# SBUF laid out anew: weight parts and moving operands at fixed places modulo 256 bytes

## The chip, the core and the metric

The kernel runs on one core of a Trainium2 chip. The metric is the device time of one execution in microseconds (us). Within the core, PE (TensorE) multiplies matrices, PEld is its weight-load side, DVE (VectorE) and ACT (ScalarE) do elementwise work, POOL (GpSimd) does a few fills, and SP (SyncE) issues the DMAs. SBUF is the on-chip memory; a place in it is given here as a byte address within each of its 128 partitions, mostly modulo 256.

## What is computed

A two-layer transformer block is followed by a second block with a convolution, a gated delta rule and one more feed-forward part, on 256 tokens of width 1024, in float32. Only the large matrix products matter here; in the reference they are plain `@`:

```python
def first_block(x, ...):
    for layer in range(DEPTH):                       # 2 layers
        xn = rms_norm(h, norm_mix_g[layer])
        mix = even_mixer(...) if layer % 2 == 0 else odd_mixer(...)   # attention, xn @ w_in, y @ w_out
        h = h + mix
        h = h + conv_gated_ffn(rms_norm(h, norm_ffn_g[layer]), ...)   # x @ w_up, conv, silu(g) * u, @ w_down
    return rms_norm(h, norm_out_g)

def second_block(x, p, ...):
    proj = h @ w_in                                  # conv branch, q, k, v, z, gates
    ...                                              # depthwise conv, gated delta rule, two output gates
    x = x + y @ w_o[i]
    x = x + (jax.nn.silu(gt) * up) @ w_down[i]       # second feed-forward part
    pl = rms_norm_2(p[i] @ w_pl_proj[i], ...)
    x = x + jax.nn.sigmoid(rms_norm_2(x, ...) @ w_pl_gate[i]) * pl
    return rms_norm_2(x, g_final)
```

## The kernel before

**Weights.** All large weights come from one flat array, piece by piece (mostly 1 MB: 8 blocks of 128 rows by 256 columns). `Weights.raw` issues the DMA into a buffer `raw`. `Weights.new` then makes two parts of it: `hi` is the piece rounded to float32r by ACT (L208), `lo` is the rest, raw minus hi, by DVE (L209). Each kind has two buffers in a pool of its own (`raw`, `hi`, `lo`); in most stages `W.more` adds a third `hi` and `lo` from the stage's pool.

**Products.** Activations are split in the same way by `split_into`; a tile such as `xs0` has for each of its blocks 256 columns of hi and 256 columns of lo. `mmA` makes three matmuls of 256 columns for each block: x-hi with weight-hi, x-lo with weight-hi, x-hi with weight-lo. There the weight part is the stationary operand (128x128, loaded by PEld before each matmul) and the activation is the moving one (256 columns). `mmB`, used by `nat`, by the last gate (`mmF`) and by `pl_proj` (`mmP`), has it the other way round: the activation stands and the weight part moves. A few pieces (`NATIVE`) are multiplied unsplit, `hg` moving against `raw`. All go through `mm`, so the profile has them on L265.

**Tiles that move in `mmA`.** `xs1` (the normalised input of the feed-forward parts and of the in-projection of the second block; the attention output in `out_proj`, there called `mmO`), `xs0` (the input of the mixers, and the unnormalised input of the first two column pairs of a feed-forward part with convolution), `hid` (the hidden layer, moving in the down product, `mmD`), `yd0`, `yd1` and `yos` (outputs of the delta rule and of the gates). `mmU` is the up product.

**Stages.** In the trace they run one after another: even mixer (1 to 148.5 us), up and down product of layer 0 (148.5 to 274.8 to 339.2), odd mixer (to 449.9), up and down of layer 1 (to 577.3 to 641.7), the second block's mixer (to 1031.8), its up and down product (to 1162.6 to 1227.1) and the last gate (to the end). The order of instructions is that of the code; it has no scheduler.

**Places.** A pool takes SBUF in the order in which pools are opened, and a tile lies behind the tile that was first asked for before it in its pool. Nothing pads them, so a tile's place modulo 256 is what the tiles before it add up to.

Of the kernel before, what the change touches and what calls it, by code (L numbers as in the profile page):

```python
# [10 lines left out]
F32 = mybir.dt.float32  # L11
FR = mybir.dt.float32r
# [39 lines left out]
def weight_spec():  # L52

    w8 = lambda n, cols: [(n, 0, 8, c, 256) for c in cols]
    halves = lambda n, k0: [(n, k0, 4, 0, 512), (n, k0, 4, 512, 512)]
    s = [("even_in", 0, 8, 1792, 68)] + w8("even_in", (1536, 1860, 2116, 2372, 2628, 2884, 3140))
    s += w8("even_in", (0, 256, 512, 768, 1024, 1280))
    s += halves("even_out", 4) + halves("even_out", 0)
    s += up_down("up0", "down0")
    s += w8("odd_in", (1544,)) + [("odd_in", 0, 8, 1536, 8)] + w8("odd_in", (1800, 2056)) + w8("odd_in", range(0, 1536, 256))  # L60
    s += halves("odd_out", 4) + halves("odd_out", 0)
    s += up_down("up1", "down1")
    first = {"g": "ba", "k": "k", "p": "qv", "z": "z", "x": "x", "y": "y"}
    col = {"a": 0, "b": 1024, "q": 2048, "k": 3072, "v": 4096, "z": 5120, "x": 6176, "y": 7200}
    piece = lambda key: w8("in2", [col[key[0]] + 256 * int(key[1])])
    for q in SEQ:
        if q[0] == "r":
            s += piece(q[1:])
        for c in first.get(q[0], ""):
            if "r" + c + q[1] not in SEQ:  # L70
                s += piece(c + q[1])
        if q == "e":
            s += [("in2", 0, 8, 6144, 32)]
        if q == "o":
            s += w8("delta_out", range(0, 1024, 256))
    s += w8("conv_out", range(0, 1024, 256))
    s += w8("o", range(0, 1024, 256))
    u = up_down("up2", "down2")
    s += u[:2] + [("pl_proj", 0, 2, 0, 1024)] + u[2:]
    s += w8("pl_gate", range(0, 1024, 256))  # L80
    return s
# [132 lines left out]
def emit(ctx, tc, A):  # L214
    nc = tc.nc
    V, S, PE = nc.vector, nc.scalar, nc.tensor
    pool = lambda name, bufs, **k: ctx.enter_context(tc.tile_pool(name=name, bufs=bufs, **k))
    cp, sp = pool("cp", 1), pool("sp", 1)
    W = Weights(nc, A["wts"], weight_spec(), pool("raw", 2), pool("hi", 2), pool("lo", 2))
    banks = {}  # L220

    def phase(stack, name, tags):
# [18 lines left out]
    h = cp.tile([128, 8, T], F32, name="h")  # L241
    for k in range(0, 8, 2):
        nc.sync.dma_start(h[:, k:k + 2], A["xT"][:, k:k + 2])
    hgp = pool("hgp", 1)
    hg = hgp.tile([128, 8, T], F32, tag="hg", name="hg")
    xp = pool("xp", 1)
    new_xs = lambda: xp.tile([128, 8, 512], FR, tag="xs0", name="xs0")
    xs1 = cp.tile([128, 8, 512], FR, name="xs1")
    acc = cp.tile([128, T], F32, name="acc")
    ones = cp.tile([128, 128], F32, name="ones")  # L250
    V.memset(ones, 1.0)
# [7 lines left out]
    C = {n: cst[:, o:o + w] for n, (o, w) in coff.items()}  # L259
    Pm = {n: gain[:, o:o + w] if o < NGAIN else par[:, o - NGAIN:o - NGAIN + w] for n, (o, w) in poff.items()}  # L260
    ident = C["ident"]


    def mm(out, lhsT, rhs, start=True, stop=True):
# [53 lines left out]
    def small(n, name, bufs=2):  # L318
        return sp.tile([128, n], F32, tag=name, name=name, bufs=bufs)
# [46 lines left out]
    def rstd_cols(*parts, eps=EPS):  # L366
        m, r = small(2, "rm"), small(2, "rs", 3)
        V.tensor_scalar(m, mean_cols(*parts), eps, None, OP.add)
        rsqrt(r, m, 2)
        return r  # L370

    def rstd_row(r):
        t = sp.tile([128, T], F32, tag="rsb", name="rsb", bufs=2)
        S.copy(t, row_bcast(r, "rb"))
        return t
# [17 lines left out]
    def pieces_A(name, xs, n, use, parts=None):  # L393

        for i in range(n):
            w = W.split(name, parts or P_ODD)
            ps = bank("mm", "mmA")
# [11 lines left out]
    def ffn(up, dn, g, conv, beside=None):  # L409
        with ExitStack() as st:  # L410
            fp = st.enter_context(tc.tile_pool(name=up, bufs=1))
            if XF:
                W.more(fp, XF, XR if conv is not None else 0)
                st.callback(lambda: setattr(W, "extra", None))
            phase(st, up + "p", {"mm": 6, "t": 2})
            def scale(dst, ps):

                V.tensor_tensor(dst.rearrange("p (m t) -> p m t", m=2), ps.rearrange("p (m t) -> p m t", m=2),
                                rb[:, None, :].to_broadcast([128, 2, T]), OP.mult)


            xu = xs1 if conv is None else new_xs()
            for k in range(8):
                split_into(xu[:, k], h[:, k], g[:, k:k + 1])
            rb = rstd_row(rstd_cols(acc))
            hid = fp.tile([128, 22, 512], FR, tag="hid", name="hid")
            for i in range(11):
                src = []
                first = i < NU and conv is not None
                for q in range(2):  # L430
                    ps = bank("mm", "mmU")
                    w = W.split(up, P_UP)
                    for m in range(2):
                        mmA(ps[:, T * m:T * m + T], w, xu if first else xs1, m)
                    src.append(ps)
                if i == 0 and beside is not None:
                    beside()
                if first and i == 0:
                    for k in range(8):
                        t = sp.tile([128, T], F32, tag="xh", name="xh", bufs=2)  # L440
                        V.scalar_tensor_tensor(t, h[:, k], g[:, k:k + 1], rb, OP.mult, OP.mult)
                        split_into(xs1[:, k], t)
                if first or conv is None:
                    for q in range(2):
                        t = fp.tile([128, 512], F32, tag=f"cv{q}" if conv is None else "sil", name="uns", bufs=2)
                        scale(t, src[q])
                        src[q] = t
                if conv is not None:
                    cw, cb = conv
                    for q in range(2):  # L450
                        a = fp.tile([128, 512], F32, tag=f"cv{q}", name="cv", bufs=2)
                        for m in range(2):
                            ch = 22 * q + 2 * i + m
                            x, y = src[q][:, T * m:T * m + T], a[:, T * m:T * m + T]
                            S.activation(y, x, AF.Identity, bias=cb[:, ch:ch + 1], scale=cw[:, 3 * ch + 2:3 * ch + 3])  # L455
                            for d in (1, 2):
                                V.scalar_tensor_tensor(y[:, d:], x[:, :T - d], cw[:, 3 * ch + 2 - d:3 * ch + 3 - d],  # L457
                                                       y[:, d:], OP.mult, OP.add)
                        src[q] = a
                s = fp.tile([128, 512], F32, tag="sil", name="sil", bufs=2)  # L460
                S.activation(s, src[0], AF.Silu)
                V.tensor_tensor(s, s, src[1], OP.mult)
                s3 = s.rearrange("p (m t) -> p m t", m=2)
                hh = hid[:, 2 * i:2 * i + 2]
                S.copy(hh[:, :, :T], s3)
                V.tensor_tensor(hh[:, :, T:], s3, hh[:, :, :T].bitcast(F32), OP.subtract)
            for i in range(4):
                ps = bank("mm", "mmD")
                k0 = 0
                for a in range(3):  # L470
                    w = W.split(dn, P_DN)

                    for m in range(2):
                        mmA(ps[:, T * m:T * m + T], w, hid, m, k0, a == 0 and m == 0, a == 2)
                    k0 += w[0].shape[1]
                residual(i, halves(ps))


    def few_columns(name, n, xs, raw, w, t, use):


        raw = W.raw(name, raw[:, :8 * n])
        w = w[:, :16 * n].rearrange("p (k n) -> p k n", k=8)
# [177 lines left out]

    with ExitStack() as st:
        ap = st.enter_context(tc.tile_pool(name="ev", bufs=1))
        if XE:
            W.more(ap, XE)
            st.callback(lambda: setattr(W, "extra", None))
# [135 lines left out]

    with ExitStack() as st:
        ap = st.enter_context(tc.tile_pool(name="od", bufs=1))
        if XO:
            W.more(ap, XO)
            st.callback(lambda: setattr(W, "extra", None))
# [90 lines left out]
    with ExitStack() as st:  # L898
# [442 lines left out]
        yds = {}  # L1341

        def yd(hd):
            if not yds:
                dls.close()
                yds["p"] = st.enter_context(tc.tile_pool(name="dq", bufs=1))
                yds[0] = hgp.tile([128, 4, 512], FR, tag="hg", name="yd0")
                yds[1] = yds["p"].tile([128, 4, 512], FR, name="yd1")
            return yds[hd // 4][:, hd % 4]
# [225 lines left out]
```

## Time and profile before

| | us |
|---|---|
| median of 3 timed runs | 1268.67 |
| all three | 1268.9, 1263.83, 1268.67 |
| the profiled execution, as timed | 1263.23 |
| its span from first to last instruction | 1261.4 |

| engine | busy us | share of span | instructions |
|---|---|---|---|
| PE | 1229.7 | 97% | 10452 |
| PEld | 1179.9 | 94% | 10452 |
| DVE | 974.5 | 77% | 1920 |
| ACT | 712.3 | 56% | 1178 |

How to read it: matmuls are pipelined, so the length that the profile gives for one (some 280 ns) is not what it costs. In a dense row of matmuls the cost of one is the distance from its start to the next start, which is read from the starts in the timeline, or from a stretch of the chain of waits divided by its count. The mean granted clock of TensorE is 0.991 of full speed; in the stages of the feed-forward parts it is 1.00 throughout.

### The profile page before, as it was taken

What the parts mean: (1) busy time and instruction counts of PE and PEld (TensorE: products, weight loads), DVE (VectorE), ACT (ScalarE), POOL (GpSimd) and SP (SyncE); (2) the same over time, 40 slices, a digit from 0 to 9 for tenths busy, and PEclk for the clock granted to TensorE, in tenths of its full rate; (3) what the DMA queues carried; (4) which work ended last, traced back from release to release, by engine and by line L of the source; (5) the groups of instructions that cost most, each with busy time, mean ns of one, the idle gap of its engine ahead of it and who ended that gap; (6) DMA issues with size and microseconds to landing.
All of it is one profiled execution on the core that took longest, in us unless ns stands there. A gap on an engine that the chain in (4) does not pass through costs nothing.

```text
span 1261.4 us, 25071 instructions
## 1 busy us (share of the span) xinstructions
PE 1229.7 (97%) x10452; PEld 1179.9 (94%) x10452; DVE 974.5 (77%) x1920; ACT 712.3 (56%) x1178; POOL 11.6 (1%) x21
## 2 busy tenths in 40 slices
PE   8999999999999999999999999999999999999997
PEld 8988999999989889999989998989999999999997
DVE  6977699885586689887559898899997778666546
ACT  4566566564365566565425488889544555444433
POOL 0000000000000000000010000000000000000000
PEclk8999999999999999999999999999999999999998
DMA  6543355555343254545425233112143555545542
GB/s 244 198 148 148 132 203 181 190 181 184 127 149 134 101 201 167 201 167 193 151 97 179 104 127 135 68 39 98 68 168 134 183 212 199 199 174 188 184 165 78
DMA packets 29345, 195.43 MB, mean 155 GB/s; under 512 B 3504, under 2 KB 4016, under 8 KB 9136
## 3 DMA queue, kind: packets, MB, share of 16 engines
q1 hardware_dynamic: 29232, 193.83, 43.2%
q8 instruction: 82, 1.34, 0.4%
q14 instruction: 31, 0.25, 0.1%
HBM read 192.77 MB, written 1.05 MB: 154 GB/s over the span
## 4 chain that ended last, share of the span: by engine, by line
PE 74%; issue 11%; DVE 4%; ACT 3%; POOL 1%; POOLq 0%; ACTq 0%; DVEq 0%
PE mmU L265 29%; PE mmD L265 15%; PE mmA L265 12%; PE mmB L265 3%; PE mmO L265 3%; PE mmF L265 2%; DVE lo L209 1%; PE sr L265 1%; ACT hi L208 1%; PE do L265 1%; PE at_y L265 1%; PE at_t L268 1%; PE at_s L265 1%; PE mc L265 0%; PE mmP L265 0%
## 5 line engine op out<-in xcount | busy, mean ns | idle before, releaser
L208 ACT CAST hi<-raw 128x1024 fp32r<-128x1024 f32 (+2 forms) x273 | 336.4, 1252 | 296.9 <-PE mmU L265 114.1
L209 DVE TENSOR_TENSOR lo<-raw,hi 128x1024 fp32r<-128x1024 f32 (+2 forms) x273 | 399.9, 1476 | 110.7 <-ACT hi L208 109.4
L265 PE MATMUL mmU<-xs,hi 128*128 128x256 f32 x2112 | 374.2, 280 | 4.4 <-DVE h L390 4.4
L265 PEld LDWEIGHTS mmU<-xs,hi 128*128 128x128 f32 x2112 | 323.8, 188 | 5.2 <-issue 3.1
L265 PE MATMUL mmU<-xs,lo 128*128 128x256 f32 x1056 | 296.5, 281 | 1.9 <-DVE lo L209 1.9
L265 PE MATMUL mmA<-xs,hi 128*128 128x256 f32 x1152 | 223.2, 290 | 0.2 <-ACT hi L208 0.2
L265 PEld LDWEIGHTS mmU<-xs,lo 128*128 128x128 f32 x1056 | 198.7, 188 | 2.4 <-DVE lo L209 2.3
L265 PE MATMUL mmD<-hid,hi 128*128 128x256 f32 x1056 | 190.2, 283 | 0.0
L265 PEld LDWEIGHTS mmA<-xs,hi 128*128 128x128 f32 x1152 | 181.3, 191 | 1.8 <-issue 0.5
L265 PE MATMUL mmA<-xs,lo 128*128 128x256 f32 x576 | 165.8, 288 | 1.2 <-DVE lo L209 1.2
L265 PEld LDWEIGHTS mmD<-hid,hi 128*128 128x128 f32 x1056 | 164.7, 192 | 0.0
L265 PE MATMUL mmD<-hid,lo 128*128 128x256 f32 x528 | 149.4, 283 | 0.0
L265 PEld LDWEIGHTS mmA<-xs,lo 128*128 128x128 f32 x576 | 109.8, 191 | 2.9 <-DVE lo L209 1.4
L1302 DVE SCALAR_TENSOR_TENSOR cv<-cpad,par,cv 128x256 f32<-128x256 f32 x240 | 107.9, 480 | 0.5
L265 PEld LDWEIGHTS mmD<-hid,lo 128*128 128x128 f32 x528 | 101.4, 192 | 0.0
L265 PE MATMUL mmB<-hi,xs 128*128 128x256 f32 x416 | 77.5, 284 | 0.9 <-DVE h L390 0.9
L457 DVE SCALAR_TENSOR_TENSOR cv<-mmU,par,cv 128x255 f32<-128x255 f32 (+1 forms) x144 | 65.1, 478 | 11.4 <-ACT cv L455 10.3
L265 PEld LDWEIGHTS mmB<-hi,xs 128*128 128x128 f32 x416 | 64.8, 190 | 1.9 <-issue 1.5
L265 PE MATMUL mmA<-hg,raw 128*128 128x256 f32 x256 | 64.5, 388 | 0.9 <-PE mmD L265 0.9
L265 PE MATMUL mmB<-lo,xs 128*128 128x256 f32 x208 | 59.1, 284 | 0.0
L265 PEld LDWEIGHTS mmA<-hg,raw 128*128 128x128 f32 x256 | 46.0, 191 | 6.1 <-PE mmD L265 1.1
L455 ACT ACTIVATE cv<-mmU,par 128x256 f32<-128x256 f32 x72 | 38.6, 558 | 20.0 <-DVE cv L457 20.0
(449 smaller groups left out, 1725.3 us busy)
## 6 DMA issues: line engine op xcount, KB each, us to landing
raw<-in_wts_dram SPq DMA_DIRECT2D x157, 1024.0 KB, 4.8
raw<-in_wts_dram SPq DMA_DIRECT2D x24, 896.0 KB, 4.5
at_l<-in_relb_dram SPq DMA_DIRECT2D x4, 384.0 KB, 9.1
h<-in_xT_dram SPq DMA_DIRECT2D x4, 256.0 KB, 3.9
out_dram<-xg SPq DMA_DIRECT2D x2, 512.0 KB, 2.6
cst<-in_cst_dram SPq DMA_DIRECT2D x1, 640.0 KB, 8.8
buf<-in_g_plp_dram SPq DMA_DIRECT2D x1, 512.0 KB, 5.0
gfin<-in_g_fin_dram SPq DMA_DIRECT2D x1, 512.0 KB, 5.2
```

The lines of the kernel that those rows point to most:

```text
L208: self.nc.scalar.copy(hi[:, a:b], r[:, a:b])
L209: self.nc.vector.tensor_tensor(lo[:, a:b], r[:, a:b], hi[:, a:b].bitcast(F32), OP.subtract)
L265: PE.matmul(out, lhsT=lhsT, rhs=rhs, start=start, stop=stop, skip_group_check=True)
L268: PE.transpose(out, in_, ident)
L455: S.activation(y, x, AF.Identity, bias=cb[:, ch:ch + 1], scale=cw[:, 3 * ch + 2:3 * ch + 3])
L457: V.scalar_tensor_tensor(y[:, d:], x[:, :T - d], cw[:, 3 * ch + 2 - d:3 * ch + 3 - d], y[:, d:], OP.mult, OP.add)
L1302: V.scalar_tensor_tensor(cv[:, k], cpad[:, k, t:t + T], cw[:, t:t + 1], cv[:, k], OP.mult, OP.add)
```

## The change

It adds `gap`, which asks a pool for a tile that nobody uses, and opens the pools in another order: the weight pools `raw`, `hi`, `lo` first, then `xp` and `hgp`, then `cp` and `sp`. `xs1` moves from `cp` to `xp`. Gaps stand before `hid`, before the first tile of the stage pools `ev`, `od` and `dq`, and elsewhere. No computation is added, removed or altered. In the built program each engine has the same instructions in the same order, with the same semaphores and the same values waited for; what differs is the addresses.

```diff
@@ emit
-    cp, sp = pool("cp", 1), pool("sp", 1)
+
+    def gap(p, n, name):
+
+        if n:
+            p.tile([128, n // 4], F32, tag=name, name=name)
+
+
     W = Weights(nc, A["wts"], weight_spec(), pool("raw", 2), pool("hi", 2), pool("lo", 2))
+    xp, hgp, cp, sp = pool("xp", 1), pool("hgp", 1), pool("cp", 1), pool("sp", 1)
+    gap(xp, 192, "xs_gap")
...
-    hgp = pool("hgp", 1)
     hg = hgp.tile([128, 8, T], F32, tag="hg", name="hg")
-    xp = pool("xp", 1)
     new_xs = lambda: xp.tile([128, 8, 512], FR, tag="xs0", name="xs0")
-    xs1 = cp.tile([128, 8, 512], FR, name="xs1")
+    xs1 = xp.tile([128, 8, 512], FR, name="xs1")
...
+    gap(sp, 96, "sp_gap")
@@ ffn
             rb = rstd_row(rstd_cols(acc))
+            gap(fp, 192, "hid_gap")
             hid = fp.tile([128, 22, 512], FR, tag="hid", name="hid")
+            gap(fp, 64, "hid_gap2")
@@ even mixer
         ap = st.enter_context(tc.tile_pool(name="ev", bufs=1))
+        gap(ap, 224, "ev_gap")
@@ odd mixer
         ap = st.enter_context(tc.tile_pool(name="od", bufs=1))
+        gap(ap, 192, "od_gap")
@@ second block, yd
                 yds["p"] = st.enter_context(tc.tile_pool(name="dq", bufs=1))
+                gap(yds["p"], 224, "dq_gap")
```

The places modulo 256 that the two built programs have:

| tile | before | after |
|---|---|---|
| `raw`, `hi`, `lo` of the pools | 96 | 128 |
| third `hi`, `lo` in the feed-forward parts | 96 | 128 |
| third `hi`, `lo` in the even, odd mixer | 128, 160 | 128, 128 |
| `xs0`, `hg`, `yd0` | 96 | 64 |
| `xs1` | 128 | 64 |
| `hid` | 96 | 64 |
| `yd1`, `yos` | 64 | 64 |

All steps inside these tiles are multiples of 256 bytes, so the distance between a moving and a stationary operand is the same, modulo 256, for all matmuls of a tile pair. Counted over the 8064 float32r matmuls of 256 columns in pieces (moving place minus stationary place):

| distance before | distance after | matmuls |
|---|---|---|
| +32 | -64 | 4224 (2784 `mmU`, 1152 `mmA`, 288 `mmO`) |
| 0 | -64 | 2592 (1584 `mmD`, 384 `mmU`, 576 `mmA`, 48 `mmO`) |
| -32 | -64 | 384 (288 `mmA` on `yd1` and `yos`, 48 `mmA`, 48 `mmO`) |
| -64 | -64 | 48 (`mmA`, one piece of the odd mixer) |
| 0 | +64 | 576 (384 `mmB`, 192 `mmF`) |
| +32 | +64 | 144 (`mmB`) |
| +64 | +64 | 96 (`mmB`) |

## Rows read from the trace of the kernel before

**Rows 1.** The page's busy times: engine, us (share of span) xinstructions.

```profile
PE 1229.7 (97%) x10452; PEld 1179.9 (94%) x10452; DVE 974.5 (77%) x1920; ACT 712.3 (56%) x1178; POOL 11.6 (1%) x21
```

**Rows 2.** The page's chain that ended last, by engine and by line.

```profile
PE 74%; issue 11%; DVE 4%; ACT 3%; POOL 1%; POOLq 0%; ACTq 0%; DVEq 0%
PE mmU L265 29%; PE mmD L265 15%; PE mmA L265 12%; PE mmB L265 3%; PE mmO L265 3%; PE mmF L265 2%; DVE lo L209 1%; PE sr L265 1%; ACT hi L208 1%; PE do L265 1%; PE at_y L265 1%; PE at_t L268 1%; PE at_s L265 1%; PE mc L265 0%; PE mmP L265 0%
```

**Rows 3.** Chain in six dense stretches: start us, us, what xcount.

```profile
279.95 20.16 PE mmD L265 x168
...
394.94 5.40 PE mmA L265 x45
400.33 5.28 PE mmB L265 x44
...
179.99 90.10 PE mmU L265 x765
...
1059.99 90.07 PE mmU L265 x772
...
1011.97 16.09 PE mmA L265 x136
```

**Rows 4.** Groups kept apart by shape: names, shapes xcount | busy us, mean ns | idle.

```profile
L265 PE MATMUL mmU<-xs,hi 128*128 128x256 f32 x2112 | 374.2, 280 | 4.4 <-DVE h L390 4.4
L265 PE MATMUL mmD<-hid,hi 128*128 128x256 f32 x1056 | 190.2, 283 | 0.0
L265 PE MATMUL mmA<-hg,raw 128*128 128x256 f32 x256 | 64.5, 388 | 0.9 <-PE mmD L265 0.9
```

**Rows 5.** PE timeline, odd mixer, distance -64: start us, us, line, names, xcount.

```profile
387.09 0.39 PE L265 MATMUL mmA<-xs,hi 128*128 128x256 f32 x2
387.32 0.28 PE L265 MATMUL mmA<-xs,lo 128*128 128x256 f32 x1
387.43 0.39 PE L265 MATMUL mmA<-xs,hi 128*128 128x256 f32 x2
...
388.11 0.39 PE L265 MATMUL mmA<-xs,hi 128*128 128x256 f32 x2
...
390.10 0.28 PE L265 MATMUL mmA<-xs,lo 128*128 128x256 f32 x1
390.21 0.40 PE L265 MATMUL mmA<-xs,hi 128*128 128x256 f32 x2
390.45 0.28 PE L265 MATMUL mmA<-xs,lo 128*128 128x256 f32 x1
...
391.61 0.28 PE L265 MATMUL mmA<-xs,lo 128*128 128x256 f32 x1
391.72 0.39 PE L265 MATMUL mmA<-xs,hi 128*128 128x256 f32 x2
391.95 0.28 PE L265 MATMUL mmA<-xs,lo 128*128 128x256 f32 x1
...
392.65 0.40 PE L265 MATMUL mmA<-xs,hi 128*128 128x256 f32 x2
...
394.06 0.40 PE L265 MATMUL mmA<-xs,hi 128*128 128x256 f32 x2
```

**Rows 6.** PE timeline, odd mixer, weight part moving at distance +64.

```profile
356.65 0.40 PE L265 MATMUL mmB<-hi,xs 128*128 128x256 f32 x2
...
357.71 0.40 PE L265 MATMUL mmB<-hi,xs 128*128 128x256 f32 x2
```

**Rows 7.** Busy by stage: from:to, us, PE PEld DVE ACT POOL (x), clock, DMA, GB/s.

```profile
148.50:274.80 126.30, 126.28 (x1063) 125.93 (x1064) 111.49 (x173) 79.59 (x101) 0.00 (x0) 1.00 0.52 185
...
641.70:1031.80 390.10, 384.18 (x3512) 359.06 (x3512) 338.88 (x779) 251.15 (x450) 10.31 (x16) 0.99 0.35 123
```

**Rows 8.** PE's waits: who for whom, us in total, times, longest us.

```profile
PE mmU L265 <- DVE lo L209: 1.9, 2, 1.3
PE mmA L265 <- DVE lo L209: 1.2, 1, 1.2
```

## The prediction

> **What bounds the kernel now.** I read the busy times first: PE has work for 97% of the span and its weight loads for 94%, DVE for 77% [rows 1]. The chain that ended last says the same by cause: 74% of it is PE, and six groups of large products alone (mmU, mmD, mmA, mmB, mmO, mmF) make 64% [rows 2]. PE hardly waits for the weight parts; the two largest such waits are 1.9 and 1.2 us in all [rows 8]. So the kernel's time is, for the most part, a number of matmuls times the distance between their starts.
>
> That distance is the thing to look at. All of these matmuls have one form (128x128 weights, 256 columns), yet their distance differs by place. In the down product 168 take 20.16 us, 120.0 ns each. In the odd mixer mmA and mmB, in pieces at distance 0 as well, take 5.40/45 and 5.28/44, again 120.0. In the up product of layer 0, at +32, it is 90.10/765 = 117.8; in the up product of the second block, at +32 too, 90.07/772 = 116.7; on `yos`, at -32, 16.09/136 = 118.3 [rows 3]. The profile's own lengths follow (280 ns for mmU, 283 for mmD), though they are no cost [rows 4]. The distance 0 is the dearest, in two stages and with either operand as the weight. I take it that the two operand streams of PE hinder each other depending on their places modulo 256. The trace does not show the mechanism, only that the cost goes with the place.
>
> One piece of the odd mixer happens to have the new distance, -64. There, in the stretch from 387.09 to 388.11, 9 matmuls take 1.02 us, 113.3 ns each. After an interruption the same piece takes 0.35 us for three (390.10 to 390.45), 117; after another 0.34 for three (391.61 to 391.95), 113; after a third 1.41 us for twelve (392.65 to 394.06), 117.5 [rows 5]. So -64 has two rates: a fast one that no other distance holds for long, and a slow one near what +32 has now. Within a dense stretch neither changed into the other; an interruption changed it. The long stretches behave likewise: mmU at +32 holds 117.8 over 765 matmuls in one stage and 116.7 over 772 in another [rows 3].
>
> **The change part by part.** No instruction, order or wait changes, and the built program has the gaps where they were meant, so there is nothing to add or remove but nanoseconds per matmul. I cost each group at both rates of -64, the slow one taken as 117.8 (it lies between 117 and 118, and the +32 row of 117.8 has far more matmuls), the fast one as 113.3. Gains in us, slow and fast:
>
> mmD, 1584 from 120.0: 2.2 ns or 6.7 ns each, 3.5 or 10.6. The 384 mmU on `xs0` and 624 mmA and mmO at distance 0: 0.8 or 2.6, and 1.4 or 4.2. mmU on `xs1` in layers 0 and 1, 1728 from 117.8: 0 or 7.8. mmU in the second block, 1056 from 116.7: a loss of 1.2, or 3.6. The 1440 mmA and mmO at +32, which sit between 116.7 and 117.8 and for which I take 117.2: a loss of 0.9, or 5.6. The 384 from -32 and 118.3: 0.2 or 1.9. mmB and mmF swap their roles, so they go to +64, not -64: one row shows it, 1.06 us for nine, 117.8 [rows 6], so 576 from 120.0 gain 1.3 either way, and 144 from +32 nothing. The unsplit products (256 halves on `hg` and `raw`, [rows 4]) stand at 0 and go to -64; their half-rate stream has no second distance in this trace, so I bound them by 256 times the 6.7 ns between 120.0 and 113.3, 1.7 us either way, and take nothing.
>
> The feed-forward parts thus give 3.5 + 0.8 + 0 - 1.2 = 3.1 us if all are slow and 10.6 + 2.6 + 7.8 + 3.6 = 24.6 if all are fast. The mixers and the last gate give 1.4 - 0.9 + 0.2 + 1.3 = 2.0 or 4.2 + 5.6 + 1.9 + 1.3 = 13.0. The first sum lies on the path whole: mmU and mmD are 44% of the chain, 555 us [rows 2], and their 4752 matmuls take 3168 times 117.6 and 1584 times 120.0, 563 us. What hides the preparation is slack on DVE: in the up product of layer 0 it is busy 111.5 of 126.3 us [rows 7]. If PE finishes that stage in 121.5 us, at the fast rate, DVE still has 10 us to spare; were that cover gone, the gain there would stop at those 111.5. In the mixers DVE is busy 338.9 of 390.1 us in the longest one [rows 7], and softmax, the delta rule and convolution stand in the same chains, so I pass on 0.7 of the second sum: 1.4 or 9.1.
>
> A rule speaks against all this. PE's two streams give 120.0 and 113.3 ns for the same tiles at different places [rows 3, 5], which looks like one disturbing the other. The Trainium skill, page "TensorE: Matmul & The Clock Gate", section "Step-by-step: what each phase is for", says that TensorE has two independent read ports into SBUF and that "Loading the next tile's weights doesn't steal SBUF read bandwidth from the running matmul." By that rule the sum of this change would be 0; this trace does not agree with it, since the distance of starts follows the places.
>
> Half of the possible: the four dense stretches at -64 were two fast and two slow. That makes (3.1 + 24.6)/2 + (1.4 + 9.1)/2 = 13.9 + 5.3 = 19.2 us. Against the profiled execution, 1263.2 us as timed (1.8 of it outside the span), that is 1244. The median of the runs is 5.4 higher, 1268.7, and gives 1249.5; of the three timed runs and the profiled one, two lie at each end. I take the middle, 1247.
>
> **The rivals.** *Nearly all fast*, 24.6 + 9.1 to 13.0 = 34 to 38 us, 1226 to 1235, middle 1231. For it: the fast rate appears at once after an interruption, and a stretch without stalls, such as 800 matmuls of an up product and the down product behind it, may keep it to its end. Against it: half of what is seen is slow.
>
> *Nearly all slow*, 3.1 + 1.4 = 4.5 us, 1259 to 1264, middle 1261. For it: +64 and +32 show 117.8 in many stretches, so that rate seems to be one that any distance but 0 can hold. Then only the removal of distance 0 pays.
>
> *Places decide nothing*, 1263 to 1269. For it: each distance goes with certain tiles and stages, so something else of them might set the rate, such as what the other engines do there. The sentence quoted above from the Trainium skill, page "TensorE: Matmul & The Clock Gate", would have it so. Against it: at distance 0 two stages and both roles show the same 120.0 [rows 3].
>
> *Slower: -64 sinks to a third, worse rate.* The longest dense stretch at -64 in the rows is twelve matmuls [rows 5]. Should it, held longer, fall to the 120.0 that distance 0 holds for 168 and more, then 1728 lose 2.2 ns, 1056 lose 3.3, 1440 lose 2.8 and 384 lose 1.7: 3.8 + 3.5 + 4.0 + 0.7 = 12.0, less the 1.3 of mmB and mmF, 10.7 us. That is 1274 to 1279. It decides where a stretch lasts much longer than that, that is in all feed-forward parts. Against it: neither rate drifts within the stretches seen.
>
> **How the numbers follow.** Chances: a mixture as forecast, 0.52; nearly all fast 0.18; nearly all slow 0.14; places decide nothing 0.06; slower 0.10. About 0.5%, 6 us, is what a measurement of this kernel can tell from no change. The mixture is faster by more than that in nearly all its spread: with one, two or three of the three feed-forward parts fast it gives about 16, 23 or 30 us, with none 8. Nearly all slow, at 4.5 us, falls on the line, so I give a third of it to faster. Faster 0.52 + 0.18 + 0.05 = 0.75, the same 0.09 + 0.06 = 0.15, slower 0.10. The range reaches from the middle of nearly all fast, 1231, to the upper end of nearly all slow, 1264; it leaves out half of 0.18 below and the slower case and part of "nothing" above. The mixture alone spans 1235 to 1260.
>
> **What the changed profile would show.** The same instruction counts on every engine and the same waits. In the down products, starts 113.3 or 117.8 ns apart, each kept over hundreds of matmuls, where 120.0 stands now. In the up products, long stretches at 113.3 in at least one of the three. mmB and mmF at 117.8. The profile's length of an mmD matmul falls below 283 ns [rows 4]. I am wrong if mmD still shows 120, if stretches at -64 drift, or if the starts come closer while PE begins to wait for `lo` from DVE, over the 3 us of now [rows 8].

## The result, and the profile after

The changed kernel takes 1254.03 us in the median of three executions (1247.33 to 1255.93), beside 1268.30 us for the kernel before in the same series; the ratio is 0.9883, 95% interval 0.9855 to 0.9912. A fourth execution of that series took 3035.48 us at full granted clock and is left out; no run shows why. A second series gave 1251.87 (nine executions, 1249.54 to 1260.39) beside 1265.27, ratio 0.9920 [0.9894, 0.9945]. So it is about 1% faster, 14.3 and 13.4 us by medians, where 19.2 had been forecast against the profiled execution. The first profiled execution, 1255.93 us with a span of 1254.1, is 7.3 us below the one of before.

The page's busy times, as in [rows 1]:

```profile
PE 1221.4 (97%) x10452; PEld 1170.0 (93%) x10452; DVE 974.2 (78%) x1920; ACT 713.6 (57%) x1178; POOL 11.6 (1%) x21
```

The counts are those of before; PE is 8.3 us less busy, its weight-load side 9.9, and the other engines differ by at most 1.3. An mmD matmul is 279 ns long by the profile, 283 before [rows 4], and PE's waits for `lo` are 1.8 us, 3.1 before [rows 8]; names as there:

```profile
L274 PE MATMUL mmD<-hid,hi 128*128 128x256 f32 x1056 | 184.4, 279 | 0.0
...
PE mmA L274 <- DVE lo L209: 1.1, 1, 1.1
...
PE mmU L274 <- DVE lo L209: 0.7, 1, 0.7
```

Where the starts lie is read from the chain that ended last, in its dense stretches, as in [rows 3] (start us, us, what, xcount):

```profile
179.94 92.93 PE mmU L274 x820
272.88 59.85 PE mmD L274 x528
...
457.91 113.18 PE mmU L274 x961
571.09 62.20 PE mmD L274 x528
...
1045.92 110.95 PE mmU L274 x942
1156.86 62.20 PE mmD L274 x528
```

All six stretches now stand at distance -64. In layer 0 it is 92.93/820 = 113.3 ns and 59.85/528 = 113.4, in layer 1 and in the second block 117.8 in each. The 120.0 of the down product has gone from all three layers. One of three feed-forward parts is at the fast pace, two at the slow one, each from the last interruption in its up product (177.8, 455.0 and 1043.6 us) to its end. The first pieces, before that, stand at either pace. The unsplit products, for which nothing was taken, stand at 216 ns before and after.

The stages of the feed-forward parts and of the second block's mixer, as in [rows 7] (from:to, us, busy PE PEld DVE ACT POOL, granted clock, DMA share, GB/s), first profile of after:

```profile
148.80:272.70 123.90, 123.47 (x1062) 123.00 (x1063) 110.91 (x172) 79.24 (x101) 0.00 (x0) 0.99 0.53 188
272.70:333.70 61.00, 60.06 (x531) 59.90 (x529) 35.12 (x48) 28.02 (x38) 0.31 (x1) 1.00 0.51 177
...
443.70:570.90 127.20, 127.13 (x1062) 126.80 (x1063) 112.28 (x175) 79.29 (x103) 0.00 (x0) 0.99 0.53 189
570.90:634.20 63.30, 62.41 (x531) 62.23 (x529) 33.32 (x50) 25.43 (x37) 0.81 (x1) 1.00 0.43 153
634.20:1025.00 390.80, 384.35 (x3513) 358.59 (x3513) 338.90 (x779) 251.81 (x450) 10.29 (x16) 0.99 0.35 123
1025.00:1156.70 131.70, 130.96 (x1086) 129.56 (x1087) 92.73 (x116) 60.08 (x60) 0.00 (x0) 1.00 0.55 190
```

Up and down product of layer 0 give 2.4 and 3.4 us, those of the other two 0.2, 1.1, -0.9 and 1.2: 7.4. The mixers and the gate give nothing in this execution (-0.1). One reason is the clock. Windows of the same view, in this profile:

```profile
150.20:153.60 3.40, 3.40 (x19) 3.40 (x18) 3.32 (x6) 3.40 (x2) 0.00 (x0) 0.52 0.03 7
443.80:447.20 3.40, 3.40 (x16) 3.29 (x17) 3.40 (x6) 3.40 (x7) 0.00 (x0) 0.51 0.62 260
706.60:713.40 6.80, 6.80 (x31) 6.53 (x31) 4.60 (x15) 2.59 (x5) 0.00 (x0) 0.51 0.00 0
```

There the granted clock was at the lower of its two levels (1.2 GHz), and matmuls started 213 ns apart. A further window of 3.4 us stands at 952.5. In the profile of before the lower level stands, in these stages, at 715.8 and at 958.1, 3.4 us each, and not at the start of the up products. The first window followed a wait of PE for `h` from DVE of 1.93 us; the second profile below has that same wait and no fall. And the first kernel under Experiments, whose up products stand where they stood before, has a window at the start of layer 1's (448.1 us). So I put it down to the execution, not to the change.

### The profile page after: what moved, and what is told of

Its sections match the earlier page's. It is cut to its first block, busy times and chain, and to the rows that moved or that the text cites. A ratio compares the mean times of both kernels' runs of the same rounds, so it can differ in the third digit from the quotient of the medians.

```text
span 1254.1 us, 25071 instructions
## 1 busy us (share of the span) xinstructions
PE 1221.4 (97%) x10452; PEld 1170.0 (93%) x10452; DVE 974.2 (78%) x1920; ACT 713.6 (57%) x1178; POOL 11.6 (1%) x21
## 4 chain that ended last, share of the span: by engine, by line
PE 72%; issue 12%; DVE 5%; ACT 3%; POOL 1%; POOLq 0%; ACTq 0%; DVEq 0%
PE mmU L274 28%; PE mmD L274 15%; PE mmA L274 12%; PE mmO L274 3%; PE mmB L274 3%; DVE lo L209 2%; PE mmF L274 2%; PE sr L274 1%; ACT hi L208 1%; PE do L274 1%; PE at_y L274 1%; PE at_t L277 1%; PE at_s L274 1%; PE mc L274 1%; ACT xbd L1191 0%
## 5 line engine op out<-in xcount | busy, mean ns | idle before, releaser
L274 PEld LDWEIGHTS mmU<-xs,lo 128*128 128x128 f32 x1056 | 202.2, 192 | 1.4 <-DVE lo L209 1.2
L274 PE MATMUL mmD<-hid,hi 128*128 128x256 f32 x1056 | 184.4, 279 | 0.0
L274 PEld LDWEIGHTS mmD<-hid,hi 128*128 128x128 f32 x1056 | 160.4, 188 | 0.0
```

The lines of the kernel that those rows point to most:

```text
L274: PE.matmul(out, lhsT=lhsT, rhs=rhs, start=start, stop=stop, skip_group_check=True)
```

## Experiments

In all of them the pace is the distance between the starts of 256-column float32r matmuls. "Fast" is 113.3 ns, "slow" 117.8. Where no spread and no interval stands beside a time, the kernel was executed once.

**One part of the change alone.** The kernel before, with gaps round `hid` only; all else as before, so the up products stay at distance 0 and +32.

```diff
+            fp.tile([128, 48], F32, tag="hid_gap", name="hid_gap")
             hid = fp.tile([128, 22, 512], FR, tag="hid", name="hid")
+            fp.tile([128, 16], F32, tag="hid_gap2", name="hid_gap2")
```

> The kernel before with one part of the change: hid alone moves, from 0 to -64 against the weights; xs1, xs0 and all else stay. If the distance sets the rate: mmD leaves 120.0 ns between starts and shows 113.3 or 117.8 in each of the three down products; mmU on xs1 stays at 117.8 or 116.7, mmA at distance 0 at 120.0; the time falls by 3.5 us (all slow) to 10.6 us (all fast). If something else of the new layout sets it (the absolute places of weights, the order of the pools): mmD stays at 120.0 and the time within 0.5%.

1255.88 us beside 1265.71. The chain, down products of layer 0, layer 1 and the second block (the middle one from 577.94 on):

```profile
276.24 59.87 PE mmD L265 x528
...
577.94 54.17 PE mmD L265 x478
...
1156.64 62.20 PE mmD L265 x528
```

113.4, 113.3 and 117.8, where before they stand at 120.0 ([rows 3] for layer 0; the stages of the other two are as long). The long stretches of the up products stay at 117.8, 118.0 and 116.7. Moving one tile, with the same instructions around it, moved the pace of its matmuls and of no other: this shows that the place decides.

**Distance or place.** After, with every tile 128 bytes higher, so the weight parts at 0 and the moving operands at 192.

```diff
+    gap(W.rawp, 64, "shift")
     xp, hgp, cp, sp = pool("xp", 1), pool("hgp", 1), pool("cp", 1), pool("sp", 1)
```

> The changed kernel with every tile 128 bytes higher: weights at 0 modulo 256, moving operands at 192, the distance still -64. If only the distance counts: the same two rates, 113.3 and 117.8 ns, in the same kinds of stretches, none at 120.0 or 116.7; which stretch gets which may differ; time 1240 to 1260 us. If the absolute place counts: other rates, or 120.0 again.

1246.51 us. The same two paces and no other: layers 0 and 1 fast, the second block slow (62.08 us for 527). The distance counts; the places themselves, shifted together, bring no new pace. One shift was tried; with the two kernels above, -64 has now shown the same two paces at three pairs of places (`hid` against weight parts: 32 and 96, 64 and 128, 192 and 0).

**Other distances, with a break ahead of each piece.** A 1-column float32 matmul, called a kick here (its result is not used), ahead of each of the 102 feed-forward weight pieces, to enter each piece anew. `hid` at -48, -80 and -64 in the three parts, `xs0` and `xs1` at -64.

```diff
+            def kick():
+                mm(bank("t", "kick")[:, 0:1], ones, ones[:, 0:1])
...
                     w = W.split(up, P_UP)
+                    kick()
```

> The changed kernel with one extra matmul of a single column ahead of each weight piece of the feed-forward parts (102 in all, some 0.2 us each with its refill, 15 to 25 us more), so that each piece of 48, 42 or 96 matmuls starts anew. hid stands at -48, -80 and -64 in the three parts. If the phase at the start of a stretch picks between two rates that then hold: the pieces of an up product, all alike in places, are a mixture of 113.3 and 117.8, each piece at one rate, where the changed kernel had some 1400 matmuls at one rate. If the rate belongs to the stage (its other engines, its buffers): all pieces of one stage keep that stage's rate. -48 and -80 show whether steps of 16 bytes matter: the same pair of rates if not.

1277.63 us. The chain of the second block's down product, at -64 (a float32 kick shows as x2; pieces have 42 or 48 matmuls):

```profile
1187.93 4.89 PE mmD L274 x42
1192.82 0.12 PE kick L274 x2
1192.94 5.76 PE mmD L274 x48
1198.70 0.12 PE kick L274 x2
1198.82 4.89 PE mmD L274 x42
1203.71 0.12 PE kick L274 x2
1203.82 5.06 PE mmD L274 x42
1208.88 0.12 PE kick L274 x2
1209.00 5.57 PE mmD L274 x48
```

Pieces are fast (4.89 for 42, 5.57 for 48) and slow (5.06, 5.76) in turn. I had taken an entry for a draw; it is not: each kick turns the pace. At -48 and -80 a piece of 42 takes 5.11, with a mean distance of starts of 119.1 and 119.2.

In the next kernel, with the same kicks, `xs0`, `xs1` and `hg` are at -96, `hid` at -96, -112 and -128, and the weight parts of mmB and mmF at +96.

```diff
-    gap(xp, 192, "xs_gap")
+    gap(xp, 160, "xs_gap")
...
-            gap(fp, 192, "hid_gap")
+            place = {"up0": -96, "up1": -112, "up2": -128}[up] % 256
```

> As the one with extra matmuls at -64, but xs0, xs1 and half of yd at -96, and hid at -96, -112 and -128 in the three parts; mmB and mmF at +96. If -64 is special: rates of 116.7 to 120.0 here and none at 113.3. If any distance away from 0 has a fast and a slow rate: 113.3 and 117.8 here too, in other shares; a distance that shows 113.3 alone would give a kernel faster than both, by some 15 us against the changed one.

1282.86 us. By starts 117.4 to 118.4 at -96, 118.5 at -112, 119.1 at -128, 119.8 at +96, each a mean over pieces of several paces, and no stretch at 113.3 at any of them. (One mmA stretch, on `yos`, which stayed at -64, is at 113.4.) Of the distances tried, -64 is the best.

**Kinds of kick.** After, with kicks as above; of three pieces two got the kind on trial, the third the 1-column float32 one.

```diff
+            tab = {"up0": (("twice", 1), ("f32", 2)), "up1": (("f32", 16), ("f32", 64)), "up2": (("fr", 128), ("fr", 64))}[up]
```

> Kernel after with a small extra matmul (its result is not used) ahead of each of the 102 FFN weight pieces. Of three pieces in a row two get the kind on trial, the third the 1-column float32 matmul that turned 113.3 into 117.8 and 117.8 into 113.3 piece by piece in the run before. On trial: two 1-column ones in a row (up product of layer 0), float32 of 2 columns (its down product), of 16 (up, layer 1), of 64 (down, layer 1), a float32r matmul of 128 columns on the piece's own weights (up, layer 2), of 64 columns (down, layer 2). Theory (the pace is a phase that an interruption shifts by a fixed amount): every kind has one answer for each pace it meets, so each either turns both paces, keeps both, or leads both to one; the third piece of each group always turns. Rival (each entry is a draw of its own): the same kind from the same pace leads now to 113.3, now to 117.8, about half and half. Under both the paces are 113.3 and 117.8 and no other, and a kick costs about 0.2 us, the longer ones up to 0.4: 1275 to 1295 us in all.

> The same with other kinds on trial: float32 of 4 columns (up, layer 0), bfloat16 of 1 column (down, layer 0), bfloat16 of 128 columns (up, layer 1), float32r of 192 columns (down, layer 1), float32 of 128 columns (up, layer 2), float32 of 8 columns (down, layer 2). Theory (fixed shift of a phase): one answer for each kind and pace met; at least one kind that leads both paces to 113.3 would be what a kernel needs to have the fast pace always. Rival (a draw): mixed answers. 1275 to 1295 us.

1273.01 and 1266.32 us, both below the 1275 to 1295 that were expected. What followed each kick that stood directly between two stretches of at least 14 float32r matmuls at -64, the kicks of the first such run (1277.63 us) counted in:

| kick | met 113.3 | met 117.8 |
|---|---|---|
| float32, 1 column | 117.8 in 71 of 71 | 113.3 in 61 of 61 |
| float32, 2, 4, 8, 16, 64 or 128 columns | 117.8 in 33 of 33 | 113.3 in 30 of 30 |
| two of 1 column in a row | 117.8 in 7 of 7 | 117.8 in 6 of 6 |
| float32r, 128 columns | 117.8 in 7 of 7 | 113.3 in 6 of 6 |
| bfloat16, 1 or 128 columns | 113.3 in 11 of 11 | 113.3 in 10 of 10 |
| float32r, 64 columns | not met | 117.8 in 4, 113.3 in 4 |
| float32r, 192 columns | 113.3 in 2 of 2 | 117.8 in 3, 113.3 in 3 |

For all but the last two rows the answer is fixed, so a draw at each entry is refuted. In the last two it was 117.8 right after a float32 kick's piece and 113.3 after the next, so the pace alone is not the whole of what is carried over. The row that matters is bfloat16: it leads to the fast pace from either. The chain of layer 0's down product with 1-column bfloat16 kicks (a single one) between float32 kicks (x2):

```profile
298.87 0.02 PE kick L274
298.89 4.89 PE mmD L274 x42
303.78 0.11 PE kick L274 x2
303.90 5.05 PE mmD L274 x42
308.95 0.02 PE kick L274
308.97 5.56 PE mmD L274 x48
314.53 0.02 PE kick L274
314.55 4.89 PE mmD L274 x42
```

A bfloat16 kick and its entry cost 0.02 + 5.56 - 48 x 0.1133 = 0.14 us.

**The changed kernel once more.** No edit.

> The changed kernel itself once more, for a second profile. Theory (the pace of an FFN part is settled by the phase at its last interruption, which differs from execution to execution): FFN parts are again at 113.3 or 117.8 throughout, but not the same ones need be fast as in the first profile (layer 0 alone); 1236 with three fast, 1243 with two, 1249 to 1255 with one, 1261 with none. Rival (which part is fast is fixed by the program): layer 0 fast, layers 1 and 2 slow again, 1252 to 1257.

> The changed kernel in several executions beside before. Theory (one of two paces per FFN part and execution): single times spread over 1235 to 1262, in steps of 5 to 6 us by the number of FFN parts that came out fast; before spreads over less than 6. Rival (a fixed pattern): all within 4 us.

1248.67 in a single execution and 1251.87 in the median of the series. The second profile (of the single execution), layer 0, layer 1 and the second block's mixer:

```profile
148.10:274.10 126.00, 125.04 (x1063) 124.56 (x1064) 111.34 (x173) 79.48 (x101) 0.00 (x0) 1.00 0.53 186
274.10:337.40 63.30, 62.36 (x531) 62.19 (x529) 34.77 (x48) 27.60 (x37) 0.31 (x1) 1.00 0.48 169
...
447.50:570.30 122.80, 121.44 (x1062) 120.98 (x1063) 111.85 (x174) 78.83 (x104) 0.00 (x0) 1.00 0.55 194
570.30:631.20 60.90, 60.01 (x531) 59.84 (x529) 33.57 (x50) 25.70 (x38) 0.78 (x1) 1.00 0.46 161
631.20:1017.70 386.50, 379.68 (x3512) 353.93 (x3512) 339.01 (x779) 251.13 (x450) 10.29 (x16) 1.00 0.36 124
```

Here layer 1 is fast and layer 0 slow; in the first profile it was the other way round, and the third profile (of the series) has layer 0 fast again, 122.5 and 60.9. So the program fixes the two paces and the execution picks. The second and the third profile come from two chips, so by themselves they leave the chip as a rival. But on one chip, too, the pace differs: the first long stretch of mmA (141 matmuls, from 31.8 us on) is at 113.3 in the third profile and at 117.8 (from 34.7 us on) in that of the steered kernel below, which ran on the same chip and has its first kick later. The nine times lie at 1249.5 to 1251.9 (five) and 1256.7 to 1260.4 (four), as one fast part and none would give; no profile shows that the clusters are these, and the clock has a share in them (mean 0.991 in the lower, 0.989 in the upper). The spread that was expected to reach down to 1235 did not: no execution shows the time of three fast parts. Nor did before stay within the 6 us that were expected: its twenty times lie at 1257.89 to 1269.27, as wide apart as those of after.

**Steering.** After, with a 1-column bfloat16 kick at three pieces of each up product, nine in all, written to the columns that the piece itself overwrites.

```diff
+    def kick(ps):
+        o = ones.bitcast(BF)
+        mm(ps[:, 0:1], o[:, :128], o[:, 0:1])
...
                     w = W.split(up, P_UP)
+                    if 2 * i + q in (2, 4, 6):
+                        kick(ps)
```

> After with a 1-column bfloat16 matmul (its result is overwritten at once) ahead of the third, fifth and seventh weight piece of each up product, 9 in all. In the run before, this kind led 113.3 to 113.3 and 117.8 to 113.3, each time, at some 0.13 us. Theory: from the third piece (in layer 0 the seventh) to the end of the down product every FFN part stands at 113.3: up near 123 us, down 60.9 in all three; against the second profile of after (1248.7, one part fast) two parts at 5.6 us each, less 9 x 0.13: 1238, the same in every execution to 4 us. Rival (the entries are a draw whatever is put ahead): parts at 117.8 in some executions, 1240 to 1262.

1239.83 us, 1239.21 to 1242.30; against before 0.9807 [0.9780, 0.9834]. All four executions are faster than every one of the thirteen of after. The six stages:

```profile
149.60:272.10 122.50, 122.16 (x1066) 121.64 (x1067) 110.75 (x172) 79.11 (x101) 0.00 (x0) 1.00 0.53 190
272.10:333.00 60.90, 59.98 (x530) 59.80 (x529) 35.05 (x48) 27.86 (x38) 0.31 (x1) 1.00 0.51 178
...
443.10:566.70 123.60, 122.37 (x1066) 121.91 (x1067) 110.42 (x174) 78.74 (x103) 0.00 (x0) 1.00 0.55 193
566.70:627.60 60.90, 60.01 (x531) 59.84 (x529) 33.59 (x50) 25.67 (x38) 0.81 (x1) 1.00 0.46 159
...
1015.50:1143.30 127.80, 127.15 (x1089) 125.52 (x1090) 92.62 (x116) 60.13 (x60) 0.00 (x0) 1.00 0.56 196
1143.30:1204.30 61.00, 60.06 (x531) 59.90 (x529) 32.79 (x40) 26.00 (x32) 0.00 (x0) 1.00 0.51 176
```

All three parts are fast, and the nine kicks, some 1.3 us, are paid for: 12.0 us less than after in the same series. Two kicks missed. The first of layer 0 (162.1 us) was followed by 117.8. It did not come behind a dense stretch, but two mmU matmuls behind other work (timeline, start us, us, as in [rows 5], idle time in brackets):

```profile
161.33 0.70 PE L274 MATMUL rb<-diag,ones 128*128 128x256 f32 x2 [0.32 <-DVE diag L374]
...
162.11 0.18 PE L274 MATMUL mmU<-ones 128*128 128x1 bf16 x1
162.15 0.48 PE L274 MATMUL mmU<-xs,hi 128*128 128x256 f32 x2
```

That seems to be the condition. Take the kicks at -64 in the profiles of this kernel and of the two further steered ones below that were followed by at least 14 matmuls in a row. Directly behind 14 or more dense matmuls, with no wait after the kick, 113.3 followed in 39 of 39; closer behind other work, 113.3 in 7 and 117.8 in 6. Why is open. The first kick of layer 1 was placed by the build at 444.9 us, before a wait, and its effect did not last; the next one, at 468.5 us, set the pace. (In the code that kick stands behind two whole pieces, 96 matmuls, in the trace behind 15: the build does move PE's instructions between neighbouring pieces, which the section on the kernel denied.)

**Steering everywhere.** The same, with kicks also ahead of the first two up pieces and of the mixers' mmA and mmB groups, some 70 more.

```diff
             ps = bank("mm", "mmB")
+            kick(ps)
```

> As the one before, and the same small matmul ahead of the first two FFN pieces, of every piece of the mixers' mmA groups and of every mmB group (moving 64 bytes above the weights): some 70 more. Theory: mmA groups go to 113.3 throughout; of the mmB groups (117.8 nearly always in after, one group at 113.3 in the second profile) more stand at 113.3 if the fast pace is a matter of entry at +64 too, none if it is not. Some 1500 mixer matmuls at on average 2.3 ns less and 400 at up to 4.4 less: -3.5 to -5.3 us, against 70 x 0.13 = 9 us of small matmuls: 1241 to 1245, so slower than with nine of them.

1245.20 us, 5.4 more than with nine. The profiled execution of it is a poor witness for the sum: its first up product holds 6.8 us at the lower clock (granted 0.97 over its 126.1 us). What it shows is the pace of mmB at +64: a kick was mostly followed by 117.8 there, by 113.3 in 4 groups.

**Kicks without the change.** Before, with the same nine kicks.

> Before with the same nine small matmuls, its addresses as they were (distance 0, +32, -32). Theory (the fast pace exists at -64 or +64 alone): no dense stretch at 113.3 in the FFNs, pieces at distance 0 still 120.0, at +32 116.7 or 117.8: 1264 to 1268, no difference beyond 0.4%. Rival (the small matmul alone brings the fast pace, the place is beside the point): FFN at 113.3, 1238.

1266.35 us, ratio 1.0017 [1.0002, 1.0032]. The down product at distance 0 stays at 120.0:

```profile
277.21 63.37 PE mmD L265 x528
```

No stretch at +32 in the up products is at 113.3 either; there two kicks between dense pieces changed 116.7 to 117.8 and 117.8 to 116.7, and two left 117.8 as it was. So +32 has two paces as well, and the fast pace needs the place; the kick only chooses between the paces that a place has.

**The other side.** The steered kernel, with `hid` of layers 0 and 1 at 64 bytes above the weight parts and a kick ahead of each output piece of the down products.

```diff
+            place = {"up0": 64, "up1": 64, "up2": -64}[up] % 256
...
                     w = W.split(dn, P_DN)
+                    if a == 0:
+                        kick(ps)
```

> The kernel with nine small bfloat16 matmuls, with hid of layers 0 and 1 moved to 64 bytes above the weights (layer 2 stays 64 below), and one more such matmul ahead of each of the four output pieces of every down product. Theory 1 (the side matters: at +64 the pace is 117.8 with hardly an exception, as the mmB groups showed): down products of layers 0 and 1 at 117.8 and 63.4 us each, that of layer 2 at 113.3 and 61.4: about 1245. Theory 2 (only the 64 bytes matter, and mmB stays at 117.8 for its being interrupted so often): all three down products at 113.3 from a small matmul on, 61.4 us each: about 1241.

1244.84 us. Stages of the three down products:

```profile
272.40:336.20 63.80, 62.86 (x535) 62.56 (x533) 35.08 (x48) 27.87 (x38) 0.31 (x1) 1.00 0.48 170
...
569.30:633.10 63.80, 62.91 (x535) 62.57 (x533) 33.56 (x50) 25.71 (x38) 0.80 (x1) 1.00 0.43 153
...
1147.00:1208.60 61.60, 60.66 (x535) 60.35 (x534) 32.80 (x40) 25.99 (x32) 0.00 (x0) 1.00 0.51 175
```

At +64 all eight kicks were followed by 117.8, at -64 all four by 113.3: 2.2 us a part. So what a bfloat16 kick leads to depends on the side, for mmD as for mmB. That mmD has no fast pace at +64 is not shown: mmB has it there at times.

## Why the prediction was right, and where it was not

*The bound, and what the change acts on.* Right: same counts, PE's busy time down, and the starts changed in the groups that were moved, the second block's mmU going from 116.7 to 117.8 in the three profiles of after, as its term for the slow case had it. The rival that places decide nothing fell with the first experiment. Read as the prediction reads it, the sentence of the Trainium skill that was quoted beside it (page "TensorE: Matmul & The Clock Gate", section "Step-by-step: what each phase is for") would have given 0 for moving `hid` alone; the trace disagrees, 120.0 to 113.4 ns for the same matmuls in layer 0.

*Two paces at -64, kept until an interruption.* Right, from a row of 9 and a row of 12 matmuls [rows 5]: in after they hold for hundreds. The slower rival, a sinking to 120.0, fell: 528 matmuls keep 113.4. mmB and mmF stood at 117.8, as one row had said [rows 6], with few exceptions.

*The sum if all are slow, 3.1 for the feed-forward parts.* Right: a slow layer 0 (second profile) gives 0.3 + 1.1, a slow layer 1 (third profile) 0.3 + 1.1, a slow second block (second profile) -1.0 + 1.2, 3.0 in all. (The mean of mmU by which it was held against the chain, 117.6, is 117.7 by its own terms.)

*The sum if all are fast, 24.6.* A little large: fast parts gave 7.3 (layer 0, third profile), 8.1 (layer 1, second profile) and, with its kicks, 6.5 (second block, steered), 21.9. Since the down products gave their full 3.5 each, the lack is in the up products, whose first two to five pieces are cut by other work and enter anew at either pace.

*The mixers and the gate, 5.3.* Of the right order: in the second profile the stages are shorter by 0.4, 0.6, 3.6 and 0.2, 4.8 in all. Part of the 3.6 is the clock, since before had two windows at the lower level there and the second profile one. Between profiles with one such window each, the second block's mixer takes 389.4 and 389.8 us at its old places (`hid` alone moved; kicks without the change) and 386.5, 386.0 and 387.9 at the new ones (after, second profile; the other side; steering), which is 1.5 to 3.8 less. In the first profile they gave -0.1, and that, with the window at the head of the up product of layer 0, is why this execution shows 7.3 and not some 14.

*Half of the possible.* This step was too large, and it carried the sum. Each of the three profiles of after has one fast part of three, and the medians say 14.3 and 13.4. For one fast part the text had "about 16", and the two profiles with no window at the lower clock in a feed-forward part gave 13.7 and 14.6 us (1249.54 and 1248.67 against 1263.23). The 19.2 took a mean of states of which no execution has the mean, from four short stretches of a mixer that were entered behind other work than the feed-forward pieces are. That it came as near as it did is in part luck: with the shifted kernel's two of three, four profiles show five fast parts of twelve, too few to tell a half from a third. The number 1247 then also leaned on the profiled execution of before, 1263.23, the lowest of its first four times. The range, 1231 to 1264, held all thirteen times that are counted.

*Nearly all fast* was priced at 1231 and had 0.18. It exists, but no execution of after reached it; with the kicks it is 1239.8. By the stages, the profile with kicks is 22.8 us shorter than that of before, where the sum had 33.7; 7.4 of the 10.9 missing are the mixers and the gate, which stay mixed, the rest the up products, with their heads and kicks.

What settles the pace where no kick stands, or where one follows other work closely (which earlier interruption counts, and what is carried over beside the pace itself), stays open, as does the mechanism behind the distances.

## What to carry to other kernels

Where matmuls run back to back, compare the distance of their starts from group to group; if it differs at one shape, look at where the moving and the stationary operand lie relative to each other modulo 256 bytes. Put the moving one 64 bytes below, see that the pace holds in more than one execution, and if a place has two paces, try a 1-column bfloat16 matmul to enter the fast one, between two dense pieces behind the last interruption (right behind other work it led to either pace here). A gain that hangs on such a state is best shown as a spread of times and several profiles, since one profile (7.3 us here) can mislead by half.

## What the runs showed of the hardware

- The pace by distance (moving minus stationary, modulo 256), 256-column float32r: -128 119.1, -112 118.5, -96 117.4 to 118.4, -80 119.2, -64 113.3 or 117.8, -48 119.1, -32 118.3, 0 120.0, +32 116.7 or 117.8, +64 117.8, +96 119.8 ns.
- +64 has the fast pace too, more rarely. In the second profile of after two mmB stretches are at 113.4, in the third one of 96 matmuls at 113.3. The longer of the two:

```profile
104.11 7.60 PE mmB L274 x67
```

- At -64, one column of float32 between two dense pieces turned the pace in 132 of 132 cases, and one column of bfloat16 led to the fast one in 47 of 47 (8 in the trial of kinds, 39 in the steered kernels); close behind other work the latter did so in 7 of 13. An added matmul can thus make a kernel faster: nine of them gave 12.0 us by medians.
